# Joined edits to a three-block transformer kernel: two matmuls for three in the down projections, token-major groups in the last block, side jobs in half steps

## The chip, the cores and the metric

The kernel runs on one core of one Trainium2 chip. The metric is the device time of one execution in microseconds. The kernel before took 1733.04 us (median of 3 runs, 1731.53 to 1735.68).

## What is computed

Three transformer blocks follow each other on one sequence of 256 tokens (272 in the first block, with 16 meta tokens) of width 1024, in fp32. Cut to what matters:

```python
# first block: latent attention, then a gated linear recurrence
h = h + mla_mixer(rmsnorm(h, a_norm_g), ...)       # 8 heads, low-rank q and kv
r = sigmoid(uc @ w_rg + b_rg); i = sigmoid(uc @ w_ig + b_ig)
log_a = -8 * r * softplus(-lam); a = exp(log_a)
mult = sqrt(-expm1(2 * log_a))                     # 1 at the first token
b = mult * (i * uc)                                # then h_t = a_t * h_(t-1) + b_t
h = h + (scan(a, b) * silu(gate)) @ w_out
# second block, two layers: sparse attention, two convolution branches, a gated sum, an ffn
x = x + merged @ w_o
x = x + (silu(u_gate) * u_val) @ w_down            # 2816 wide
# third block
ret = silu(rg) * retention(rq, rk, rv)             # normalised per head of 256
mix = sigmoid(ga) * (ret @ w_ret_out) + sigmoid(gb) * (moba_attention(mq, mk, mv) @ w_moba_out)
x = x + mix @ w_o
x = x + (silu(h2 @ w_ffn_gate) * (h2 @ w_ffn_up)) @ w_ffn_down
```

## The kernel before

**Precision.** Weights and activations are fp32, and each is split into a high part of TensorE's fast type and a low rest. A product is then three matmuls (mm3): high by high, low weight by high activation, high weight by low activation. ScalarE (ACT) makes the high part of every piece of weight (whi, L175), VectorE (DVE) the rest (wlo, L181); in some stages a DMA issued by GpSimd (POOL) makes the rest instead.

**Units.** Weights come in units of 128x1024 elements (512 KB), in the order in which they are used. A dry run of the program records that order; in the second, a unit is loaded, and its split emitted, three units ahead of its use (AHEAD = 3).

**Two layouts of a product.** Feature-major (tile_fm): the weight's 128x128 piece is the stationary operand and 256 or 272 tokens move; one unit (8 pieces over k) makes one output tile of 128 features, in 24 matmuls of 256 columns. Token-major (tok_group, proj_tok): the activation's 128 tokens are stationary and 512 weight columns move; a unit holds two k, and makes 12 matmuls of 512 columns into two accumulators, one for each half of the tokens. Transposes on TensorE (to_fm, L858) bring a token-major result back.

**Side jobs.** Everything that is no large product (norms, heads of an attention, convolution taps) is a Python generator. `spawn` starts one with a rate; each unit of the main products calls `tick`, which advances every job by its rate in steps; `drain` runs a job to its end at once. `stagger` runs several heads at once, each some steps behind the other. An instruction's place on its engine's queue is then set by the scheduler of the tile framework; the queues run in order.

**The places that the change touches.** (1) `residual` runs an output projection over 8 tiles and adds it to x; called for the down projections of the two layers with kt = 22 k-pieces (w_dn), whose operands are fz, three pairs of tiles fh and fl. The third block's down projection (w_d3, L1543) is written out apart. (2) `mla`: heads are advanced at L655 to L670, then w_a_out starts with `lead`, the first k-pieces of four tiles, and `between` drains the heads. (3) `lru`, the recurrence: `block` makes the gates r and i by Sigmoid (L719), `gates` does Exp (L709) and Tanh (L711), a Sqrt over two tiles follows (L725), and `chain` multiplies on DVE (L740) and on POOL (L743) and scans (L747). (4) `third`: w_g3 makes the gate of the retention (8 tiles) and the two mixing gates (8 tiles each) feature-major, each scaled by the row rb of inverse norms; `retain` transposes its heads (L1466); `moba` makes the attention's heads from transposed probabilities (pt, ptb) and v (mo, L1418).

```python
    def tick(self, n=1.0):
        for job in list(self.jobs):
            job[2] += job[1] * n
            while job[2] >= 1.0 and job in self.jobs:
                job[2] -= 1.0
                self.step(job)
```

## Time and profile before

| | |
|---|---|
| median of 3 runs | 1733.04 us |
| profiled execution: its own time | 1733.38 us |
| its span (first to last instruction) | 1731.3 us |
| TensorE (PE) busy | 1709.9 us, 99% |
| DVE busy | 1365.5 us, 79% |
| ACT busy | 1068.0 us, 62% |
| POOL busy | 61.7 us, 4% |
| granted TensorE clock, mean | 0.999 |

Matmuls are pipelined: a row says 0.28 us for a matmul of 256 columns, but the next one starts 0.12 us later. What a matmul costs in a stream is the distance from its start to the next one's start, and that is read from a timeline or from a first and a last start with their count. "busy" can hide short gaps for the same reason; the waits are read from the view of waits and from the timeline.

### The profile page before, as it was taken

What the parts mean: (1) busy time and instruction counts of PE and PEld (TensorE: products, weight loads), DVE (VectorE), ACT (ScalarE), POOL (GpSimd) and SP (SyncE); (2) the same over time, 40 slices, a digit from 0 to 9 for tenths busy, and PEclk for the clock granted to TensorE, in tenths of its full rate; (3) what the DMA queues carried; (4) which work ended last, traced back from release to release, by engine and by line L of the source; (5) the groups of instructions that cost most, each with busy time, mean ns of one, the idle gap of its engine ahead of it and who ended that gap; (6) DMA issues with size and microseconds to landing.
All of it is one profiled execution on the core that took longest, in us unless ns stands there. A gap on an engine that the chain in (4) does not pass through costs nothing.

```text
span 1731.3 us, 31869 instructions
## 1 busy us (share of the span) xinstructions
PE 1709.9 (99%) x12215; PEld 1622.9 (94%) x12215; DVE 1365.5 (79%) x2943; ACT 1068.0 (62%) x1808; POOL 61.7 (4%) x92
## 2 busy tenths in 40 slices
PE   9999899999999999999999999999999999999999
PEld 8999899998888999999999888999998789999999
DVE  7769998998997998667998898898757677786553
ACT  5667775677656776546578557576545756455442
POOL 1000100000000000000000000000000000000000
PEclk9999999999999999999999999999999999999999
DMA  7425465776775555667686775656665436656563
GB/s 271 135 71 170 133 204 177 218 221 195 230 227 176 191 180 181 184 175 210 190 228 196 214 222 189 202 171 197 186 191 187 146 96 187 189 163 196 184 184 97
DMA packets 91545, 318.64 MB, mean 184 GB/s; under 512 B 10448, under 2 KB 11616, under 8 KB 91392
## 3 DMA queue, kind: packets, MB, share of 16 engines
q1 hardware_dynamic: 84384, 292.51, 53.1%
q0 software_dynamic: 7008, 24.09, 7.0%
q8 instruction: 96, 1.57, 0.4%
q14 instruction: 57, 0.47, 0.1%
HBM read 293.96 MB, written 1.05 MB: 170 GB/s over the span
## 4 chain that ended last, share of the span: by engine, by line
PE 92%; ACT 3%; DVE 2%; issue 1%; DMA 1%; SPq 0%; DVEq 0%; POOLq 0%; ACTq 0%
PE acc L205 22%; PE acc L207 22%; PE acc L206 21%; PE tok L207 7%; PE tok L205 7%; PE tok L206 7%; DVE wlo L181 1%; ACT whi L175 1%; PE lg L1115 1%; PE ix L1070 1%; PE po L1108 1%; DMA wlo<-raw 1%; ACT ca L1234 0%; DMA raw<-w_a_in 0%; PE pt L913 0%
## 5 line engine op out<-in xcount | busy, mean ns | idle before, releaser
L175 ACT ACTIVATE whi<-raw 128x1024 fp32r<-128x1024 f32 (+3 forms) x573 | 586.4, 1027 | 417.1 <-PE acc L207 170.3
L181 DVE TENSOR_TENSOR wlo<-raw,whi 128x1024 fp32r<-128x1024 f32 (+3 forms) x531 | 628.3, 1186 | 203.6 <-ACT whi L175 199.3
L205 PE MATMUL acc<-bh,whi 128*128 128x256 f32 x1600 | 459.1, 288 | 0.0
L206 PE MATMUL acc<-bh,wlo 128*128 128x256 f32 x1600 | 451.7, 283 | 0.0
L207 PE MATMUL acc<-bl,whi 128*128 128x256 f32 x1600 | 451.2, 283 | 0.0
L205 PEld LDWEIGHTS acc<-bh,whi 128*128 128x128 f32 x1600 | 306.8, 192 | 2.7 <-issue 1.4
L206 PEld LDWEIGHTS acc<-bh,wlo 128*128 128x128 f32 x1600 | 306.6, 192 | 2.2 <-issue 0.7
L207 PEld LDWEIGHTS acc<-bl,whi 128*128 128x128 f32 x1600 | 306.1, 192 | 0.2 <-DVE bl L158 0.2
L979 DVE SCALAR_TENSOR_TENSOR ca<-apad,vec,ca 128x226 f32<-128x226 f32 (+14 forms) x480 | 195.9, 460 | 0.3
L206 PE MATMUL acc<-ah,wlo 128*128 128x256 f32 (+1 forms) x528 | 151.5, 287 | 6.1 <-DVE wlo L181 6.1
L205 PE MATMUL acc<-ah,whi 128*128 128x256 f32 (+1 forms) x528 | 153.3, 290 | 1.5 <-ACT ah L161 1.1
L207 PE MATMUL acc<-al,whi 128*128 128x256 f32 (+1 forms) x528 | 151.5, 287 | 0.0
L205 PE MATMUL acc<-fh,whi 128*128 128x256 f32 x528 | 149.4, 283 | 0.0
L206 PE MATMUL acc<-fh,wlo 128*128 128x256 f32 x528 | 149.4, 283 | 0.0
L207 PE MATMUL acc<-fl,whi 128*128 128x256 f32 x528 | 149.4, 283 | 0.0
L206 PEld LDWEIGHTS acc<-ah,wlo 128*128 128x128 f32 x528 | 101.2, 192 | 7.1 <-DVE wlo L181 7.0
L205 PEld LDWEIGHTS acc<-ah,whi 128*128 128x128 f32 x528 | 101.2, 192 | 2.3 <-ACT ah L161 1.3
L205 PE MATMUL tok<-whi,ah 128*128 128x424 f32 (+1 forms) x272 | 102.7, 377 | 0.0
L205 PEld LDWEIGHTS acc<-fh,whi 128*128 128x128 f32 x528 | 101.4, 192 | 0.0
L206 PEld LDWEIGHTS acc<-fh,wlo 128*128 128x128 f32 x528 | 101.4, 192 | 0.0
L207 PEld LDWEIGHTS acc<-fl,whi 128*128 128x128 f32 x528 | 101.4, 192 | 0.0
L207 PEld LDWEIGHTS acc<-al,whi 128*128 128x128 f32 x528 | 101.1, 192 | 0.2 <-DVE al L162 0.2
(559 smaller groups left out, 3332.8 us busy)
## 6 DMA issues: line engine op xcount, KB each, us to landing
raw<-w_up SPq DMA_DIRECT2D x88, 512.0 KB, 3.9
raw<-w_g SPq DMA_DIRECT2D x72, 512.0 KB, 4.4
raw<-w_c SPq DMA_DIRECT2D x48, 512.0 KB, 4.5
raw<-w_f SPq DMA_DIRECT2D x44, 512.0 KB, 3.6
wlo<-raw POOLq DMA_DIRECT2D x36, 512.0 KB, 6.6
raw<-w_t SPq DMA_DIRECT2D x40, 424.0 KB, 3.2
raw<-w_a SPq DMA_DIRECT2D x32, 512.0 KB, 4.4
raw<-w_dn SPq DMA_DIRECT2D x32, 512.0 KB, 3.6
```

The source lines that it names most:

```text
L175: nc.scalar.activation(hi[:, c], raw[:, c], AF.Copy)
L181: nc.vector.tensor_sub(lo[:, c], raw[:, c], hi[:, c].bitcast(F32))
L205: mm(out, wh, xh, start=start, stop=False)
L206: mm(out, wl, xh, start=False, stop=False)
L207: mm(out, wh, xl, start=False, stop=stop)
L979: tap = dve.scalar_tensor_tensor(ca[:, i, d:], ga[:, i, :T - d], w(i, j), ca[:, i, d:], op0=ALU.mult, op1=ALU.add)
L1070: te.matmul(ps[:, n * 2 * nk:(n + 1) * 2 * nk].rearrange("p (h k) -> p h k", h=2), kiT[:, 2 + i, q], kiT[:, 6:8, :nk], start=True, stop=True)
L1108: te.matmul(po, tok[k][:, 584 + g * 128:584 + (g + 1) * 128], ptb[:, k * n:(k + 1) * n], start=k == 0, stop=k == j)
L1115: te.matmul(ps[:, i * nk:(i + 1) * nk], qT[:, h, q], kiT[:, g, :nk], start=True, stop=True)
```

## The change

Seven edits, made together:

1. The three down projections issue two matmuls for each k-piece where there were three: the high weight by high and low activation side by side (512 columns, into the two halves of a bank), and the low weight by the high activation (256 columns, into the first half). The two halves are then added by two DVE additions where there was one. The activation's parts are stored in pairs (class Pairs) for it.
2. In the third block, w_g3, w_mo and w_ro are token-major; the inverse norm is then a scale for each partition in the activation that empties the accumulator, and the row rb isn't made. The retention stays token-major (ry), is multiplied by its gate, and is transposed after that; the mixed sum is transposed too (mixture), before w_o3, which starts with `lead=(4, 4)`.
3. proj_tok and tok_group call `tick(0.5)` after each k instead of `tick()` after each two.
4. One `step(heads)` less ahead of w_a_out.
5. In `lru`, Sigmoid is written as a Tanh of half the argument, with the factors moved into scales and biases; the product of L743 moves from POOL to DVE.
6. The second sum of rows of the latent norm takes an accumulator of the products' pool instead of the pool of one tile.
7. In the third block, the first group of projections is emptied only after the norm's job is drained.

```diff
+    def wide_part(self, o, unit, xs, k0, k1, kt, base=0):
+        wh, wl = unit
+        mm = self.nc.tensor.matmul
+        for k in range(k0, k1):
+            x = xs(k)
+            c = slice((k - base) * 128, (k - base + 1) * 128)
+            mm(o, wh[:, c], x, start=k == 0, stop=k == kt - 1, skip_group_check=True)
+            mm(o[:, 0], wl[:, c], x[:, 0], start=False, stop=k == kt - 1, skip_group_check=True)
+        self.tick((k1 - k0) / 8)
...
-                r = yield from self.rows(r6[:, 3 * a:3 * a + 3], SEG1, "rb_l%d" % a)
+                r = yield from self.rows(r6[:, 3 * a:3 * a + 3], SEG1, "rb_l%d" % a,
+                                         self.acc("rlp") if a else None)
...
         self.step(heads)
-        self.step(heads)
         self.residual("w_a_out", 8, lambda k: (oh[:, k], ol[:, k]), h, T1, 0, ["b_norm_g"],
                       lead=(4, 5), between=lambda: self.drain(heads))
...
+            if wide:
+                o = next(first) if m < nl else self.wide_fm(name, m, kt, xw, n)
+                dve.tensor_add(src, o[:, 1], src)
+                o = o[:, 0]
...
-                dst, b = (rr, "b_b_rg") if c < 2 else (ii, "b_b_ig")
-                self.late(act.activation(dst[:, i], o, AF.Sigmoid, bias=self.v(b, i)))
+                dst, b = (rr, 0) if c < 2 else (ii, 8)
+                self.late(act.activation(dst[:, i], o, AF.Tanh, scale=0.5,
+                                         bias=self.hb[:, b + i:b + i + 1]))
...
-                dve.memset(rr[:, i, 0:1], 1.0)
-                pool.tensor_mul(ii[:, i], ii[:, i], rr[:, i])
+                dve.memset(rr[:, i, 0:1], 0.5)
+                dve.tensor_mul(ii[:, i], ii[:, i], rr[:, i])
...
                     self.mm3(a[j], xh[:, s], xl[:, s], wh[:, c], wl[:, c], k == 0, k == kt - 1)
-            self.tick()
+                self.tick(0.5)
...
-            pt = self.acc("rt")
-            for i in range(2):
-                for j in range(2):
-                    te.transpose(pt[:, i * 256 + j * 128:i * 256 + j * 128 + 128],
-                                 y[:, j * 256 + i * 128:j * 256 + i * 128 + 128], self.ident)
...
+        for g in range(2):
+            o = self.tok_group("w_g3", g, 8, xs)
+            for j in range(2):
+                act.activation(gr[:, j, g * 512:g * 512 + 512], o[j], AF.Copy,
+                               scale=self.rcol[:, j:j + 1])
...
+            for m in range(0, 8, 2):
+                c = slice(m * 128, m * 128 + 256)
+                dve.tensor_mul(ry[:, :, c], ry[:, :, c], gr[:, :, c])
                 yield
+                self.to_fm(ry, m, rT_h, rT_l)
+                yield
...
+        self.residual("w_o3", 8, lambda k: (mh[:, k], ml[:, k]), x, T, 0, ["norm2_w_3"],
+                      lead=(4, 4), between=lambda: self.drain(rjob))
...
-            o = self.tile_fm("w_d3", m, 22,
-                             lambda k: (fz[k // 8][0][:, k % 8], fz[k // 8][1][:, k % 8]), T)
-            dve.tensor_add(x[:, m], o, x[:, m])
+            o = self.wide_fm("w_d3", m, 22, lambda k: fz[k // 8](k % 8), T)
+            dve.tensor_add(x[:, m], o[:, 1], x[:, m])
+            dve.tensor_add(x[:, m], o[:, 0], x[:, m])
```

What this does to the order on the engines, at three places. The first is DVE in the recurrence, from the second product of L740 to the first weight rest behind it. Before (uc is the scan's result, gy the gate branch, ii and rr the gates):

```order
L740 SCALAR_TENSOR_TENSOR rr<-aa,rr 128x272 x2
L742 MEMSET rr 128x1
L747 SCALAR_TENSOR_TENSOR uc<-aa,ii 128x272
L742 MEMSET rr 128x1
L740 SCALAR_TENSOR_TENSOR rr<-aa,rr 128x272
L747 SCALAR_TENSOR_TENSOR uc<-aa,ii 128x272
L712 TENSOR_TENSOR ii<-ii,uc 128x272 x2
L742 MEMSET rr 128x1
L747 SCALAR_TENSOR_TENSOR uc<-aa,ii 128x272
L181 TENSOR_TENSOR wlo<-raw,whi 128x1024
```

And on the same engine at the same place of the changed kernel (L802 is the product of L740, L805 the one that was on POOL, L809 the scan, L197 the weight's rest):

```order
L802 SCALAR_TENSOR_TENSOR rr<-aa,rr 128x272
L833 TENSOR_TENSOR gy<-acc,nb_1934 128x256
L805 TENSOR_TENSOR ii<-ii,rr 128x272
L804 MEMSET rr 128x1
L802 SCALAR_TENSOR_TENSOR rr<-aa,rr 128x272
L805 TENSOR_TENSOR ii<-ii,rr 128x272
L772 SCALAR_TENSOR_TENSOR ii<-ii,uc 128x272 x2
L809 SCALAR_TENSOR_TENSOR uc<-aa,ii 128x272 x2
L197 TENSOR_TENSOR wlo<-raw,whi 128x1024
```

Two scans stand ahead of the weight's rest where there were three, and one product of L740 less; two products that POOL did stand there instead.

The second is TensorE near the end of the third block's attention, in the last group of projections (pt are transposes of probabilities, mo the product with v that needs their copy). Before:

```order
L205 MATMUL tok<-whi,ah 128x512
L206 MATMUL tok<-whi,al 128x512
L207 MATMUL tok<-wlo,ah 128x512
L913 MATMUL pt<-ident,p 128x128 x2
L1418 MATMUL mo<-ptb,rotmv 128x256
L913 MATMUL pt<-ident,p 128x128
```

In the changed kernel, from the same transposes on:

```order
L975 MATMUL pt<-ident,p 128x128 x2
L221 MATMUL tok<-whi,ah 128x512
L222 MATMUL tok<-whi,al 128x512
L223 MATMUL tok<-wlo,ah 128x512
L221 MATMUL tok<-whi,ah 128x512
L222 MATMUL tok<-whi,al 128x512
L223 MATMUL tok<-wlo,ah 128x512
L1488 MATMUL mo<-ptb,rotmv 128x256
```

Six matmuls of 512 columns stand between the transposes and the product where there were none; at the other pairs there are five to seven.

The third is TensorE at the start of w_a_out (acc<-oh is its product, pa and pb transposes of a head, po the head's product with v). Before:

```order
L590 MATMUL pa<-ident,p_1348 128x128
L598 MATMUL po<-pt_1459,qv 128x256
L599 MATMUL po<-pt,vt 128x256
L600 MATMUL po<-pt,vt 128x128
L586 MATMUL pb<-ident,p_1424 128x128
L588 MATMUL pa<-ident,p_1424 128x128
L205 MATMUL acc<-oh,whi 128x272
```

In the changed kernel:

```order
L641 MATMUL pa<-ident,p_1350 128x128
L221 MATMUL acc<-oh,whi 128x272
L222 MATMUL acc<-oh,wlo 128x272
L649 MATMUL po<-pt_1461,qv 128x256
L223 MATMUL acc<-ol,whi 128x272
```

The head's first product moved behind two matmuls of w_a_out; the second, third and the next head's transposes come twelve matmuls of it later.

## Rows read from the trace of the kernel before

**Rows 1.** The page's busy times: engine, us busy, share of the span, instructions.

```profile
PE 1709.9 (99%) x12215; PEld 1622.9 (94%) x12215; DVE 1365.5 (79%) x2943; ACT 1068.0 (62%) x1808; POOL 61.7 (4%) x92
```

**Rows 2.** The chain that ended last, share of the span by engine.

```profile
PE 92%; ACT 3%; DVE 2%; issue 1%; DMA 1%; SPq 0%; DVEq 0%; POOLq 0%; ACTq 0%
```

**Rows 3.** Waits of PE in the whole span: us in total, times, longest.

```profile
PE acc L206 <- DVE wlo L181: 6.9, 5, 3.1
PE mo L1418 <- ACT ptb L917: 3.0, 2, 1.6
PE acc L207 <- DVE yl L162: 1.3, 1, 1.3
...
PE po L598 <- DVE pt L594: 0.9, 1, 0.9
```

**Rows 4.** Instructions on fh from 1663.5 us on: durations, first and last start.

```profile
L205 PE MATMUL acc<-fh,whi x176: 283/283/283, 1664.1 to 1727.1; 128*128 128x256 f32 x176
```

**Rows 5.** Timeline of PE in w_ao of layer 1: start, us, instruction.

```profile
1007.66 0.39 PE L206 MATMUL tok<-whi,ol 128*128 128x512 f32 x1
...
1010.84 0.39 PE L205 MATMUL tok<-whi,oh 128*128 128x512 f32 x1
```

**Rows 6.** Timeline of PE from w_co to w_o of layer 0.

```profile
551.89 0.39 PE L207 MATMUL tok<-wlo,ch 128*128 128x512 f32 x1
552.12 0.28 PE L205 MATMUL acc<-mh,whi 128*128 128x256 f32 x1
552.23 0.28 PE L206 MATMUL acc<-mh,wlo 128*128 128x256 f32 x1
```

**Rows 7.** Timeline of PE around transposes in w_o of layer 0.

```profile
557.87 1.04 PE L858 MATMUL tr<-ident,mg 128*128 128x128 f32 x8
558.66 0.36 PE L205 MATMUL acc<-mh,whi 128*128 128x256 f32 x1
558.86 0.28 PE L206 MATMUL acc<-mh,wlo 128*128 128x256 f32 x1
```

**Rows 8.** Windows in the recurrence: us, then busy of PE, PEld, DVE, ACT, POOL; clock, DMA.

```profile
175.00:216.00 41.00, 33.96 (x260) 32.59 (x259) 37.25 (x71) 30.52 (x50) 7.84 (x8) 0.96 0.40 129
185.00:190.00 5.00, 4.82 (x28) 4.83 (x29) 3.86 (x9) 4.81 (x10) 0.00 (x0) 0.66 0.63 195
```

**Rows 9.** Timeline in the recurrence, DVE and POOL.

```profile
198.55 0.44 DVE L740 SCALAR_TENSOR_TENSOR rr<-aa,rr 128x272 f32<-128x272 f32 x1
...
198.79 0.83 POOL L743 TENSOR_TENSOR ii<-ii,rr 128x272 f32<-128x272 f32 x1 [14.75 <-ACT whi L175]
198.90 1.02 DVE L740 SCALAR_TENSOR_TENSOR rr<-aa,rr 128x272 f32<-128x272 f32 x1
...
202.34 1.77 DVE L181 TENSOR_TENSOR wlo<-raw,whi 128x1024 fp32r<-128x1024 f32 x1
...
204.38 1.21 DVE L181 TENSOR_TENSOR wlo<-raw,whi 128x1024 fp32r<-128x1024 f32 x1
```

**Rows 10.** Timeline at the recurrence's first wait, DVE and PE.

```profile
178.03 0.43 DVE L740 SCALAR_TENSOR_TENSOR rr<-aa,rr 128x272 f32<-128x272 f32 x1
...
182.78 0.71 DVE L747 TENSOR_TENSOR_SCAN uc<-aa,ii 128x272 f32<-128x272 f32 x1
...
183.41 1.71 DVE L181 TENSOR_TENSOR wlo<-raw,whi 128x1024 fp32r<-128x1024 f32 x1
...
185.18 0.38 PE L206 MATMUL acc<-ah,wlo 128*128 128x256 f32 x1 [1.88 <-DVE wlo L181]
```

**Rows 11.** A group of table loads of ACT, 155 to 215 us.

```profile
L719 ACT ACT_TABLE_LOAD x2 | 2.6, 1283 | 0.0
```

**Rows 12.** Timeline of PE in the third block's attention.

```profile
1376.71 0.38 PE L913 MATMUL pt<-ident,p 128*128 128x128 f32 x2
...
1378.88 0.70 PE L1418 MATMUL mo<-ptb,rotmv 128*128 128x256 f32 x2 [1.36 <-ACT ptb L917]
```

**Rows 13.** Timeline of the end: the last addition.

```profile
1727.66 0.42 DVE L1546 TENSOR_TENSOR x<-acc,x 128x256 f32<-128x256 f32 x1 [7.49 <-PE acc L207]
```

More of the change, by code (lines that the diff above doesn't have):

```diff
@@ L72, in __exit__, with __init__, __call__, parts @@
         return False
+class Pairs:
+    def __init__(self, prog, name, t):
+        self.a = [prog.big(name + "%d" % i, 8, t, F32R) for i in range(2)]
+    def __call__(self, k):
+        i = 2 * (k % 4)
+        return self.a[k // 4][:, i:i + 2]
+    def parts(self, k):
+        i = 2 * (k % 4)
+        return self.a[k // 4][:, i], self.a[k // 4][:, i + 1]
 class Prog:
@@ L224, in tile_fm, with wide_fm, wide_lead @@
         return o
+    def wide_part(self, o, unit, xs, k0, k1, kt, base=0):
[7 more added lines that the diff above has]
+        self.tick((k1 - k0) / 8)
+    def wide_fm(self, name, m, kt, xs, t):
+        o = self.acc()[:, :2 * t].rearrange("p (a t) -> p a t", a=2)
+        for k0 in range(0, kt, 8):
+            k1 = min(kt, k0 + 8)
+            self.wide_part(o, self.unit(name, m, k0 * 128, (k1 - k0) * 128), xs, k0, k1, kt, k0)
+        return o
+    def wide_lead(self, name, ms, xs, t, ks, between=None):
+        os = [(self.acc()[:, :2 * t].rearrange("p (a t) -> p a t", a=2),
+               self.unit(name, m, 0, 1024)) for m in ms]
+        for o, u in os:
+            self.wide_part(o, u, xs, 0, ks, 8)
+        if between:
+            between()
+        for o, u in os:
+            self.wide_part(o, u, xs, ks, 8, 8)
+            yield o
     def lead_fm(self, name, ms, xs, t, ks, between=None):
@@ L682, in residual @@
         nl = lead[0] if kt == 8 else 0
-        first = self.lead_fm(name, range(nl), xs, n, lead[1], between)
+        wide = isinstance(xs, list)
+        if wide:
+            xw = lambda k: xs[k // 8](k % 8)
+            first = self.wide_lead(name, range(nl), xw, n, lead[1], between)
+        else:
+            first = self.lead_fm(name, range(nl), xs, n, lead[1], between)
         for m in range(8):
-            o = next(first) if m < nl else self.tile_fm(name, m, kt, xs, n)
             src = x[:, m, t0:]
+            if wide:
+                o = next(first) if m < nl else self.wide_fm(name, m, kt, xw, n)
+                dve.tensor_add(src, o[:, 1], src)
+                o = o[:, 0]
+            else:
+                o = next(first) if m < nl else self.tile_fm(name, m, kt, xs, n)
             dve.tensor_add(src, o, src)
@@ L1333, in third, with group @@
         t1 = [self.big("t1_%d" % j, 1, 2048)[:, 0] for j in range(2)]
-        def group(g):
+        os = []
+        def group(g, wait=True):
             if g < 4:
@@ L1482, in norm @@
             self.norm_cols("n31")
-            yield
-            return (yield from self.rows(self.rcol, SEG2, "rb31"))
         job = self.spawn(norm(), 0.7)
-        group(0)
+        group(0, wait=False)
+        self.drain(job)
+        evict(0)
         group(1)
-        rb = self.drain(job)
         ajob = self.spawn(attention(), 1.2)
@@ L1514, in third @@
         mh, ml = self.big("mh", 8, T, F32R), self.big("ml", 8, T, F32R)
+        mixed = [0]
         for b, (wn, kt) in enumerate((("w_mo", 4), ("w_ro", 8))):
             ys = (lambda k: (rT_h[:, k], rT_l[:, k])) if b else (lambda k: (bT_h[:, k], bT_l[:, k]))
-            for m in range(8):
-                o = self.tile_fm("w_g3", 16 - 8 * b + m, 8, xs, T)
-                g = self.small("g3")[:, :T]
-                dve.tensor_mul(g, o, rb)
-                act.activation(g, g, AF.Sigmoid)
-                if b == 0 and m == 0:
+            for g in range(2):
+                c = slice(g * 512, g * 512 + 512)
+                o = self.tok_group("w_g3", 4 - 2 * b + g, 8, xs)
+                sgs = [self.half_k("sgt") for _ in range(2)]
+                for j in range(2):
+                    act.activation(sgs[j], o[j], AF.Sigmoid, scale=self.rcol[:, j:j + 1])
+                if b == 0 and g == 0:
@@ L1534, in third @@
-        fz = [(self.big("fh", 8, T, F32R), self.big("fl", 8, T, F32R)) for _ in range(3)]
+                if b == 1 and g == 0:
+                    self.drain(rjob)
+                    rjob = self.spawn(self.mixture(mg, mixed, mh, ml))
+                o = self.tok_group(wn, g, kt, ys)
+                for j in range(2):
+                    if b == 0:
+                        dve.tensor_mul(mg[:, j, c], o[j], sgs[j])
+                    else:
+                        dve.tensor_mul(sgs[j], o[j], sgs[j])
+                        dve.tensor_add(mg[:, j, c], mg[:, j, c], sgs[j])
@@ L1536, in finish @@
+                mixed[0] = b * (g + 1)
+        self.residual("w_o3", 8, lambda k: (mh[:, k], ml[:, k]), x, T, 0, ["norm2_w_3"],
+                      lead=(4, 4), between=lambda: self.drain(rjob))
+        fz = [Pairs(self, "f", T) for _ in range(3)]
         def finish(og, ou, i):
@@ L1686, in pack @@
                                     w[:, 1024:2048]], 1), 512)
[L1687 to L1689 removed]
+    d["w_g3"] = _tm(np.concatenate([w[:, 2048:3072], w[:, 4608:6656]], 1), 512)
+    d["w_ro"] = _tm(a["w_ret_out_3"][0], 512)
+    d["w_mo"] = _tm(a["w_moba_out_3"][0], 512)
     d["w_o3"] = _fm(a["w_o_3"][0])
```

74 lines of the change are left out of this document (30 added, 44 removed).

## The prediction

> **What bounds the kernel now.** I read the page's busy times and the chain first: PE is busy 99% of the span and is 92% of the chain, DVE is busy 79%, ACT 62% [rows 1, 2]. So the reader should see a kernel whose time is TensorE's stream of matmuls plus the gaps in that stream, and expect an edit to count only if it shortens the stream or closes a gap. The view of waits gives the gaps: 6.9 us for weight rests that DVE makes, 3.0 us for copied probabilities in the third block's attention, 1.3 us for the gated operand yl, 0.9 us in the first block's heads [rows 3]. Then I read what one matmul costs in the stream. In the last down projection 176 steps of three matmuls start between 1664.1 and 1727.1 us: 63.0 us over 175 steps is 0.360 us a step, 0.120 us for a matmul of 256 columns [rows 4]. In a token-major group 14 matmuls start between 1007.66 and 1010.84 us: 3.18 / 14 = 0.227 us for 512 columns [rows 5]. The 256 columns more cost 0.107 us, so about 13 ns of each matmul do not depend on its columns.
>
> **The down projections.** There are 528 k-pieces: 3 projections, 8 tiles, 22 pieces; rows 4 hold the last 176. A step was 0.360 us; with one matmul of 512 and one of 256 columns it is 0.227 + 0.120 = 0.347 us. 528 x 0.013 = 6.9 us less. This supposes that widths can alternate freely; where the trace has one change from 512 to 256, the wide one takes 0.23 us and the next 0.11 us [rows 6], so nothing is added there. The second addition in each tile is DVE work beside TensorE, which needs 22 x 0.347 = 7.6 us a tile, against 0.42 us for an addition [rows 13]; only the last tile's is on the path: +0.4 us.
>
> **Token-major in the third block.** w_g3 has 24 units, w_ro 8 and w_mo 8 half units: 36 units. One was 24 x 0.120 = 2.88 us and is 12 x 0.227 = 2.72 us. 36 x 0.156 = 5.6 us less. The mixed sum is now transposed, 16 transposes more; 8 of them take 0.79 us to the next matmul [rows 7], so +1.6 us. The gated heads keep their 16. The sum of rows for rb falls away, two small matmuls: I take 0.4 us, by four passes of a transpose's length.
>
> **Switches.** The first split matmul after a transpose takes 0.20 us where a stream has 0.12 [rows 7]. By the order of PE there are 14 more switches between split matmuls and others, so 7 more returns: 0.6 us at 0.08 each, 1.4 us at the whole 0.20. I take 1.0 us.
>
> TensorE's stream is then shorter by 6.9 + 5.6 - 1.6 + 0.4 - 1.0 = 10.3 us.
>
> One rule speaks against this. The Trainium skill, "TensorE: Matmul & The Clock Gate", section "Back-to-back issue gap", gives a lone matmul N / 2.4 + 2.5 ns at the full clock, a fixed part of 2.5 ns where the rows here leave 13 ns. By it the 528 matmuls saved in the down projections and the 432 in the third block would be worth an estimated 2.4 us in place of 12.5 us. The trace does not agree: by the page 256 columns would take 109 ns, and they take 120 ns.
>
> **The recurrence.** From 175 to 216 us PE is busy 33.96 of 41 us, DVE 37.25 [rows 8]. Three weight rests and the operand yl come late; the waits are most of the 6.9 us and all of the 1.3 us [rows 3]. After the first one the granted clock is 0.66 over 185 to 190 us [rows 8]: two thirds of that stretch at the lower level, 1.2 GHz, which costs 0.34 of 5 us, 1.7 us. What is late is DVE: beside a POOL product the same DVE product takes 1.02 us for 0.44 us, and a weight rest 1.77 us for 1.21 us [rows 9], about 0.55 us each; POOL makes eight products, so 8 x 0.55 = 4.4 us of DVE go when they move. They come back as eight DVE products at 0.35 us from start to start [rows 9]: 2.8 us. DVE is 1.6 us better off. ACT loads tables three times less (the order has 21 loads for 24), 3 x 1.28 = 3.8 us [rows 11], so the roots that DVE waits for come earlier.
>
> At the first wait the order tells more. The rest that PE needs starts 5.38 us after the second product of L740, at 183.41 us [rows 10]. Now that product, six other operations at 0.35 and two scans at 0.63 us (182.78 to 183.41) stand ahead, 3.7 us; so it starts 1.7 us earlier, and ends 0.5 us earlier again since no POOL product runs beside it. That covers the 1.88 us of PE's wait [rows 10], if ACT is in time. The later ones improve less, since DVE is nearly full: at the last operand three more small products stand ahead of yl. All gaps here, the waits and the slow clock, are at most 6.9 + 1.3 + 1.7 = 9.9 us; if DVE simply stays full, nothing of it goes. I take 3.5 us: 1.8 of the first wait, half of the slow clock, and 0.9 of the rest.
>
> **The third block's attention.** Two waits of the mo product cost 3.0 us [rows 3]. In one the transposes start at 1376.71 and the product at 1378.88 us [rows 12]: 2.17 us, in which ACT copies. Nothing of the main stream stood between. Now six matmuls do, 6 x 0.227 = 1.36 us, so of 1.36 us of wait nearly all is covered there. ACT is the engine that could take it back; I take 2.4 us, bounds 0 and 3.0.
>
> **The heads of the first block.** The product po waited 0.9 us [rows 3]. Now two matmuls stand ahead of it and twelve behind it, ahead of the parts that need later copies. I take 0.6 us, bounds 0 and 0.9.
>
> **Edits at nothing.** Half ticks in the two middle layers: none of PE's larger waits stands in their token-major groups [rows 3], and DVE is 21% idle over the span [rows 1]; without that cover a tap of the convolution placed ahead of a weight rest would cost its own length. The latent norm's second accumulator: it removes a wait for a buffer, worth less than what I can tell. Emptying the first group later: what is queued behind it on ACT is the split of units three ahead, 3 x 2.7 us of cover. Fewer and larger loads of w_mo: none of PE's larger waits is for a load [rows 3].
>
> **The sum.** -10.3 - 3.5 - 2.4 - 0.6 + 0.4 = -16.4 us. The profiled execution took 1733.4 us (span 1731.3 and 2.1 us around it), 0.3 us above the median: 1717.0 us.
>
> **The rivals.**
> *The waits stay.* DVE remains full in the recurrence and ACT in the attention, so that only the stream shortens: 1733.4 - 10.3 + 0.4 = 1723.5 us. For it: DVE is busy 37.25 of 41 us and gains only 1.6 us [rows 8, 9]. Against: the first wait is a matter of order, and the order is better.
> *All the waits go.* The recurrence gives 9.9 us, the attention 3.0, the heads 0.9: 1733.4 - 10.3 - 13.8 + 0.4 = 1709.7 us. For it: both full engines get relief. Against: DVE's share.
> *The fixed part isn't paid by the matmul.* The 13 ns could belong to something that the merged matmul pays as well, such as reading its operand; then a wide step stays at 0.360 us and a group gains nothing: 1717.0 + 12.5 = 1729.5 us. Against: 0.227 us for 512 columns is not twice 0.120 us [rows 4, 5]. The page's rule lies close to this case.
> *Alternating widths cost (slower).* No row shows a stream in which 512 and 256 columns take turns on one bank. If each change of width cost what the return from transposes costs, 0.08 us [rows 7], 2 x 528 changes would cost 84 us: 1717.0 + 84 = 1801 us. It decides from 16.4 / 1056 = 16 ns a change on. Against: one change at no cost [rows 6].
> *The merge does nothing.* If the three matmuls were bound by the weight's stream and not by TensorE, fewer of them would change nothing; PE's 99% and the short list of waits leave little room for it.
>
> **How the numbers follow.** The forecast case 0.60, with its own range 1713 to 1721 us. The waits stay 0.18, all go 0.11, fixed part not saved 0.05, alternating widths 0.03, no effect 0.03. A change is told from none by about 0.2%, 3.5 us. Faster: the first four cases, 0.94. Same: 0.03. Slower: 0.03. The range takes in the second and third case, 1709 to 1725 us, and leaves out 0.11.
>
> **What would show it.** Down projections: 0.347 us a k-piece, 61.0 us for the last 8 tiles where there were 63. Third block: 128x512 rows at 0.227 us for w_g3, w_mo and w_ro, 32 more transposes of tr less 16 of rt. Recurrence: L740's product at 0.44 us throughout, four table loads, no stretch at a clock under 0.9, waits on weight rests in the whole span of 4 to 5 us in place of 6.9. Attention: no wait of mo over 0.5 us. It would be wrong if the wide step took 0.36 us or more, or if a new wait stood in the third block's mixing, where DVE now sums 512 columns at a time and w_o3 waits for the transposes.

## The result and the profile after

The changed kernel took 1721.01 us (median of 4 runs, 1720.09 to 1722.51), the kernel before 1733.52 us beside it (4 runs, 1731.53 to 1735.68): a ratio of 0.9931, 95% interval 0.9919 to 0.9943. So the change is faster by 12.5 us, 3.9 us less than the 16.4 us that the sum gave: inside the stated range, 1709 to 1725 us, and at the upper end of the forecast case's own, 1713 to 1721 us. The profiled execution spans 1719.0 us, 12.3 us less than the one before, so the two profiles tell the same story as the runs. Of all the runs below one, of the kernel with two steps of the heads, took 2065.87 us where its others took 1721 to 1725, and is left out as slow.

The page of the changed kernel, busy times and then the shares of the chain, which answer to [rows 1, 2]:

```profile
PE 1704.5 (99%) x11267; PEld 1574.2 (92%) x11267; DVE 1360.6 (79%) x2922; ACT 1065.0 (62%) x1784; POOL 54.5 (3%) x84
...
PE 90%; ACT 4%; DVE 3%; DMA 1%; issue 1%; SPq 0%; POOLq 0%; ACTq 0%; DVEq 0%
```

TensorE still bounds the kernel, with 948 matmuls fewer; a per cent or two of the chain went from it to ACT and DVE.

To see where the time went I took the starts of the same matmuls in both traces (the first product on a new operand of the main stream, or the first of a norm's sum) and wrote down how much less time the changed kernel took between them:

| stretch | forecast, us | changed kernel |
|---|---|---|
| start to the norm ahead of the recurrence (heads, latent norm) | -0.6 | -0.8 |
| that norm to the norm behind the recurrence | -3.5 | -4.6 |
| layers 0 and 1 outside the down projections | 0 | +1.7 |
| three down projections | -6.9 | -3.5 |
| third block from its first projection to its last norm | -5.8 | -5.3 |
| last addition | +0.4 | +0.4 |

The third block's forecast is -5.6 + 1.6 - 0.4 + 1.0 - 2.4. Before rounding the rows add up to the 12.3 us of the span. Two of them missed: the down projections gave half, and layer 0 took back 1.7 us where nothing was expected. The recurrence gave 1.1 us more than expected in this execution.

TensorE's waits over the whole span, as in [rows 3]:

```profile
PE acc L223 <- DVE yl L178: 2.5, 1, 2.5
PE acc L221 <- ACT ah L177: 1.2, 1, 1.2
...
PE acc L221 <- ACT oh L177: 0.8, 1, 0.8
PE tok L223 <- DMA wlo<-raw: 0.8, 2, 0.5
PE acc L222 <- DVE wlo L197: 0.7, 2, 0.5
PE mups L1271 <- DVE lnst L1049: 0.5, 1, 0.5
...
PE mo L1488 <- ACT ptb L979: 0.2, 1, 0.2
```

The waits that the forecast closed are nearly closed: weight rests of DVE fell from 6.9 to 0.7 us in the products by feature, mo from 3.0 to 0.2, and po isn't in the list. The operand yl grew from 1.3 to 2.5 us, the wait for rests that a DMA makes from 0.2 to 0.8 us, and one for oh of 0.8 us is new.

The down projection of layer 0 in the changed kernel, instructions on f and then some in order of time (start, us, instruction):

```profile
L250 PE MATMUL acc<-f,whi x176: 395/398/403, 700.8 to 762.6; 128*128 128x512 f32 x176
L251 PE MATMUL acc<-f,wlo x176: 277/281/284, 701.0 to 762.8; 128*128 128x256 f32 x176
```

```profile
704.17 0.28 PE L251 MATMUL acc<-f,wlo 128*128 128x256 f32 x1
704.28 0.40 PE L250 MATMUL acc<-f,whi 128*128 128x512 f32 x1
704.52 0.28 PE L251 MATMUL acc<-f,wlo 128*128 128x256 f32 x1
704.64 0.40 PE L250 MATMUL acc<-f,whi 128*128 128x512 f32 x1
704.88 0.28 PE L251 MATMUL acc<-f,wlo 128*128 128x256 f32 x1
```

From 704.17 to 704.88 us are two k-pieces: 0.355 us each. Over the 176 pieces, from the first wide start to the first product of the next stage, it is 62.19 us, 0.3534 us a piece: a wide matmul is followed after 0.236 us and a narrow one after 0.117 us on the mean. Forecast were 0.227 and 0.120. No wait stands between them, so the 0.006 us is a price of the stream itself.

The recurrence, in windows of the stretch of [rows 8] (us; busy of PE, PEld, DVE, ACT, POOL; clock, DMA):

```profile
175.00:190.00 15.00, 15.00 (x128) 15.00 (x127) 14.96 (x35) 14.95 (x28) 0.00 (x0) 1.00 0.44 127
190.00:200.00 10.00, 9.94 (x83) 9.53 (x81) 9.98 (x22) 9.96 (x15) 0.00 (x0) 1.00 0.52 164
200.00:204.00 4.00, 1.04 (x3) 0.44 (x3) 4.00 (x11) 1.50 (x3) 0.00 (x0) 1.00 0.94 322
204.00:208.00 4.00, 3.98 (x20) 3.98 (x21) 4.00 (x12) 1.09 (x3) 0.00 (x0) 0.57 0.10 41
208.00:212.00 4.00, 4.00 (x36) 4.00 (x35) 3.40 (x6) 0.75 (x2) 0.00 (x0) 1.00 0.49 128
```

Up to 200 us TensorE now has almost no gap. DVE is full up to 208 us, and what it is late with stands at the end: TensorE has 1.04 us of work from 200 to 204 us, and after that pause the granted clock is 0.57, most of 204 to 208 us at the lower level, 1.2 GHz.

### The profile page after: what moved, and what is told of

Same layout as the page of the kernel before. It is cut to its first block, busy times and chain, and to the rows that moved or that the text cites. A ratio compares the mean times of both kernels' runs of the same rounds, so it can differ in the third digit from the quotient of the medians.

```text
span 1719.0 us, 29881 instructions
## 1 busy us (share of the span) xinstructions
PE 1704.5 (99%) x11267; PEld 1574.2 (92%) x11267; DVE 1360.6 (79%) x2922; ACT 1065.0 (62%) x1784; POOL 54.5 (3%) x84
## 4 chain that ended last, share of the span: by engine, by line
PE 90%; ACT 4%; DVE 3%; DMA 1%; issue 1%; SPq 0%; POOLq 0%; ACTq 0%; DVEq 0%
PE acc L221 16%; PE acc L223 16%; PE acc L222 16%; PE tok L223 9%; PE tok L221 9%; PE tok L222 9%; PE acc L250 7%; PE acc L251 4%; DVE wlo L197 1%; ACT whi L191 1%; PE lg L1177 1%; PE ix L1132 1%; PE po L1170 1%; DMA wlo<-raw 1%; ACT ca L1296 0%
## 5 line engine op out<-in xcount | busy, mean ns | idle before, releaser
L197 DVE TENSOR_TENSOR wlo<-raw,whi 128x1024 fp32r<-128x1024 f32 (+3 forms) x527 | 626.7, 1192 | 207.5 <-ACT whi L191 202.2
L250 PE MATMUL acc<-f,whi 128*128 128x512 f32 x528 | 186.7, 399 | 0.0
L251 PE MATMUL acc<-f,wlo 128*128 128x256 f32 x528 | 148.3, 281 | 0.0
L221 PE MATMUL tok<-whi,ah 128*128 128x512 f32 (+1 forms) x368 | 142.4, 387 | 0.0
L223 PE MATMUL tok<-wlo,ah 128*128 128x512 f32 (+1 forms) x368 | 138.3, 376 | 0.0
L222 PE MATMUL tok<-whi,al 128*128 128x512 f32 (+1 forms) x368 | 138.0, 375 | 0.0
L250 PEld LDWEIGHTS acc<-f,whi 128*128 128x128 f32 x528 | 99.2, 188 | 24.7
L251 PEld LDWEIGHTS acc<-f,wlo 128*128 128x128 f32 x528 | 99.7, 189 | 0.0
L221 PE MATMUL acc<-ah,whi 128*128 128x272 f32 (+1 forms) x336 | 98.1, 292 | 1.2 <-ACT ah L177 1.2
L222 PE MATMUL acc<-ah,wlo 128*128 128x272 f32 (+1 forms) x336 | 97.1, 289 | 0.3 <-DVE wlo L197 0.2
L223 PE MATMUL acc<-al,whi 128*128 128x272 f32 (+1 forms) x336 | 96.9, 288 | 0.0
```

The source lines that it names most:

```text
L197: nc.vector.tensor_sub(lo[:, c], raw[:, c], hi[:, c].bitcast(F32))
L221: mm(out, wh, xh, start=start, stop=False)
L222: mm(out, wl, xh, start=False, stop=False)
L223: mm(out, wh, xl, start=False, stop=stop)
L250: mm(o, wh[:, c], x, start=k == 0, stop=k == kt - 1, skip_group_check=True)
L251: mm(o[:, 0], wl[:, c], x[:, 0], start=False, stop=k == kt - 1, skip_group_check=True)
```

## The experiments

The ratios are to runs of the kernel before on the same chip (medians 1732.2 to 1733.4 us). "c" is the first product on the convolution's output, "z" that on the attention's output of a middle layer; from z to c lie w_so, its gates, w_ao and the side work of the convolution. The landing of a DMA is the time from its issue until its data have arrived.

### Widths in blocks

```diff
-            mm(o[:, 0], wl[:, c], x[:, 0], start=False, stop=k == kt - 1, skip_group_check=True)
+        for k in range(k0, k1):
+            c = slice((k - base) * 128, (k - base + 1) * 128)
+            mm(o[:, 0], wl[:, c], xs(k)[:, 0], start=False, stop=k == kt - 1,
+               skip_group_check=True)
```

> The changed kernel, with the eight wide products of a unit first and its eight narrow ones behind them, so that the width changes twice in a unit and not sixteen times. In the changed kernel a down projection takes 62.19 us, 0.3534 us a k-piece, where I had 0.347; the wide start is followed after 0.236 us, the narrow one after 0.117 us. Theory 'changing width costs': wide 0.227 to 0.230 and narrow 0.120, 0.347 to 0.350 us a piece, 61.1 to 61.6 us a projection, 1.8 to 3.4 us less in all: 1717.6 to 1719.2 us. Rival 'this wide product costs 0.236 us wherever it stands' (its operand of two rows, or its output): 0.236 + 0.120 = 0.356 us, 62.6 us a projection, 1722 us.

Measured: 1718.58 us (1717.72 to 1723.76), ratio 0.9924 [0.9912, 0.9937]. A projection takes 61.49 us, 0.70 us less, in all three of them. The same view as above, of this kernel:

```profile
L250 PE MATMUL acc<-f,whi x176: 389/393/398, 700.2 to 760.7; 128*128 128x512 f32 x176
L253 PE MATMUL acc<-f,wlo x176: 277/283/283, 702.0 to 761.6; 128*128 128x256 f32 x176
```

So the width's changes cost, and the rival falls. The starts show how: in each of the 72 blocks, to within 2 ns, the intervals from the first wide matmul on are 233, 236, 228, 233, 231, 227, 227 and 227 ns, and from the first narrow one 113, 119 and then 120 ns. The price sits behind a change from 256 to 512 columns, 26 to 28 ns over five matmuls, and the change back returns 8 ns. The trace of the kernel before had it, at the start of the third block, where the last down projection ends:

```profile
1301.11 0.28 PE L207 MATMUL acc<-fl,whi 128*128 128x256 f32 x1
1301.23 0.40 PE L205 MATMUL tok<-whi,ah 128*128 128x512 f32 x1
1301.47 0.40 PE L206 MATMUL tok<-whi,al 128*128 128x512 f32 x1
1301.70 0.39 PE L207 MATMUL tok<-wlo,ah 128*128 128x512 f32 x1
1301.93 0.40 PE L205 MATMUL tok<-whi,ah 128*128 128x512 f32 x1
1302.16 0.39 PE L206 MATMUL tok<-whi,al 128*128 128x512 f32 x1
1302.39 0.39 PE L207 MATMUL tok<-wlo,ah 128*128 128x512 f32 x1
```

From 1301.23 to 1302.39 us five matmuls take 1.16 us where the settled cadence gives 5 x 0.227 = 1.135.

### Fewer changes of width

This kernel also uses half ticks in the third block alone, as a run below does.

```diff
-        for k in range(k0, k1):
...
+        for w in ((0, 1), (1, 0))[k0 // 8 % 2]:
+            for k in range(k0, k1):
+                c = slice((k - base) * 128, (k - base + 1) * 128)
+                if w == 0:
+                    mm(o, wh[:, c], xs(k), start=k == 0, stop=k == kt - 1, skip_group_check=True)
+                else:
+                    mm(o[:, 0], wl[:, c], xs(k)[:, 0], start=False, stop=k == kt - 1,
+                       skip_group_check=True)
```

> As the run before last of the wide products (blocks by unit, half ticks in the third block alone), with the order of the second unit of a tile turned round: wide, narrow, narrow, wide, wide, narrow. In the block order the intervals behind a change from 256 to 512 columns are 233, 236, 228, 233 and 231 ns, then 227; behind a change from 512 to 256 they are 113 and 119 ns, then 120. So a pair of changes costs 26 to 28 ns and gives 8 back. Theory 'each pair of changes costs about 20 ns': three pairs a tile become two, 8 x 0.020 = 0.16 us less a projection, 61.33 us in place of 61.49, 0.5 us in all: 1716.6 us. Rival 'the pattern goes by the place in the unit and not by the change': 61.49 us stays.

Measured: 61.33 us for each of the three projections, as the theory had it to the digit. The median is 1719.10 us (1717.71 to 1720.09), ratio 0.9921 [0.9907, 0.9934], not the 1716.6 expected: in its profile layer 0 takes 1.6 us more than in the kernel it is compared with, a loss that the next point follows.

### Ticks by halves and by wholes

In both token-major helpers, for the changed kernel with whole ticks (and with the signs turned for the kernel before with half ticks):

```diff
-                self.tick(0.5)
+            self.tick()
```

> The changed kernel, with the side jobs advanced by whole units again in both token-major helpers. The changed kernel loses 1.75 us between 478 and 525 us in w_so and its gates of layer 0, where rests made by a DMA of POOL's queue land 8.1 to 10.2 us after their issue; layer 1 loses nothing at the same place. Theory 'the half ticks put the side work so that the DMA's transfer or its issue comes late': no wait for a DMA's rest there, 1.75 us back; and in the third block's attention the product mo waits about 1.4 to 2.4 us again, so about the same time in all, 1721 to 1722 us. Rival 'the kernel comes there 5.5 us earlier, and the transfers meet others': the 1.75 us stay, 1722 to 1723 us. Rival 'landing times differ from run to run': either.

> The kernel before, with only the half ticks. Theory 'half ticks cost in layer 0': 1 to 2 us lost between w_ao and w_co of layer 0, with waits for rests made by a DMA, none in layer 1, and the waits of mo in the third block's attention (3.0 us) fall to under 1 us, since products of the main stream now stand between its transposes and mo: 1731 to 1733 us. Rival 'earlier arrival': nothing lost in layer 0, 1731 us. Rival 'the attention's gain comes from the token-major blocks around it and not from the half ticks': mo still waits 2 to 3 us.

The third block first. The wait of mo in the changed kernel with whole ticks, and in the kernel before with half ticks:

```profile
PE mo L1488 <- ACT ptb L979: 3.0, 2, 1.6
```

```profile
PE mo L1418 <- ACT ptb L917: 0.2, 1, 0.2
```

The half ticks alone close that wait. Put into the kernel before they shorten the span by 2.1 us, 2.0 of it between the third block's first projection and the end of its attention, and the time is 1729.97 us (1729.21 to 1732.0), ratio 0.9985 [0.9977, 0.9994]. Taken from the changed kernel they cost 1.7 us there: 1723.17 us (1720.7 to 1725.16), ratio 0.9943 [0.9929, 0.9956]. The rival, that the token-major blocks did it, falls.

In layer 0, from z to c, the changed kernel takes 116.07 us and the kernel before 114.32. With whole ticks it is 114.55 us, and with the half ticks in the kernel before 114.08: neither alone makes the loss. The next two runs carry this on.

```diff
-                self.tick(0.5)
+                if self.fine:
+                    self.tick(0.5)
+            if not self.fine:
+                self.tick()
...
+        self.fine = True
```

> The changed kernel, with the wide products of a unit ahead of its narrow ones, and half ticks in the third block alone. The block order gave 0.70 us a projection, 2.1 us. Theory 'half ticks cost in layer 0 and help in the third block': 114.0 to 114.5 us between the two marks of layer 0 in place of 115.55 us, and mo waits 0.2 us: 1.0 to 1.5 us less than with the block order alone, 1717.3 us. Rival 'landing of the DMA's rests differs from run to run': 114.0 to 116.1 us, and 1718.6 us.

Measured: 1717.07 us (1716.22 to 1720.61), ratio 0.9911 [0.9898, 0.9924], with 114.01 and 114.03 us from z to c in the two layers: the shortest time of all. That fits the theory of the half ticks, but the kernel of the turned order has the same ticks, and its layer 0 takes 115.65 us. So I ran the changed kernel once more:

> The changed kernel once more, unchanged, for what differs from run to run. In its trace the rests made by DMA in w_so and the gates of layer 0 land 9.6 and 10.2 us after their issue, and the stretch takes 116.07 us; in a kernel where they land within 8.7 us it takes 114.0 us, and in one with the same half ticks within 8.6 us 114.1 us. Theory 'the landing differs from run to run, and the half ticks only leave less room': another time than 116.07 us, between 114.1 and 116.1, with landing times that go with it. Rival 'the order fixes it': 115.9 to 116.2 us again. Time 1721 us, within 1.

Measured: 1722.65 us (1720.45 to 1724.08), ratio 0.9939 [0.9927, 0.9952]. The same kernel's two medians, 1721.01 and 1722.65 us, are 1.6 us apart, so a smaller difference between two medians here says little. Layer 0 takes 114.59 us this time, and layer 1, which had lost nothing, 116.79 us. So the loss isn't fixed by the order of instructions. It goes with the landing of the rests made by DMA. The rows of that DMA's issue line give their count and their time to landing; the changed kernel, layer 0:

```profile
L195 POOL DMA_DIRECT2D wlo<-raw x5: 869/869/869, 444.7 to 488.2; - x5
...
DMA to landing us min/median/max: 5.0/8.1/10.2
```

the same kernel once more, layer 1:

```profile
L195 POOL DMA_DIRECT2D wlo<-raw x4: 872/872/874, 989.3 to 1023.1; - x4
...
DMA to landing us min/median/max: 8.5/9.5/9.7
```

and the one that lost nothing, layer 0:

```profile
L196 POOL DMA_DIRECT2D wlo<-raw x5: 872/872/872, 445.5 to 489.0; - x5
...
DMA to landing us min/median/max: 4.5/7.6/7.8
```

In the two layers 0 they are issued at the same moments after z; in layer 1 the first of them is, and the others come 0.8 to 1.4 us later, behind its late landing. With units split three ahead, in no layer whose longest landing is 9.3 us or less is more than 0.3 us lost against 114.03; with 9.6 and 10.2 us for the last two it is 2.0 us, with 9.8 and 10.6 us (turned order) 1.6 us. Of the 2.0 us the view of waits gives 0.8 to these rests; by the starts of the products the units that wait for them lose 1.4 us, since the matmuls behind a wait start late as well, and 0.6 us is lost at the norm's sum that comes behind them (the row lnst above).

It is not a matter of POOL's queue alone: the load of w_g issued 0.2 us behind the last of these rests lands after 10.6 us in the changed kernel and after 5.1 us in the one that lost nothing, and the three loads ahead of it were issued 0.3 to 1.2 us before that rest in the first and 2.4 to 3.3 us before it in the second. That fits transfers that slow each other when they come close together, and a late landing that pushes the next loads later; no run varied it.

What starts it stays open: four profiles of the kernel before and its variants have no stretch over 114.32 us, eight of nine of the changed kernel and its variants have one over 114.5, with whole ticks as with half. That may be more than chance, but no single part of the change explains it.

### More lead for the rests

```diff
-    AHEAD = 3
+    AHEAD = 4
```

> The kernel with block order and half ticks in the third block alone (1717.07 us), with weight units split four ahead of the one in use in place of three; a unit of the token-major stages takes 24 x 0.227 = 5.4 us. Over ten profiles of the changed kernel and its variants, the stretch from z to c of layers 0 and 1 takes 114.0 to 116.8 us and goes with the landing of the rests made by DMA: within 9 us of their issue nothing is lost, at 9.6 to 10.6 us 0.6 to 2.7 us. Theory 'the loss is that lateness alone': with 5.4 us more lead 114.0 to 114.3 us in both layers and no wait of TensorE for such a rest, whatever the landing; over several executions some 0.5 to 1.5 us less than before in this stretch. Against it in the sum: the rests that DVE makes stand one unit earlier in its queue, and in the recurrence, where DVE is busy 14.98 of 15 us, the operand yl can come 1 to 2 us later. Time 1716 to 1719 us. Rival 'the split waits for the buffer of the unit in use': no earlier issue, the waits stay, 1717 us or more.

Measured: 1724.44 us (1723.9 to 1725.79), ratio 0.9957 [0.9943, 0.9970]: 7 us slower than with three. In layer 0:

```profile
L196 POOL DMA_DIRECT2D wlo<-raw x5: 869/869/869, 449.4 to 492.9; - x5
...
DMA to landing us min/median/max: 4.6/5.9/6.2
```

and the waits of TensorE over the span:

```profile
PE tr L1125 <- DVE tok L952: 2.2, 2, 1.3
PE tok L222 <- ACT ch L174: 1.4, 2, 0.7
...
PE tok L223 <- DVE cl L175: 1.0, 2, 0.5
```

The waits for the DMA are gone, but not by more lead. These are the first products on z in layer 0 of the kernel with three ahead and of this one:

```profile
409.61 0.47 PE L222 MATMUL tok<-whi,zh 128*128 128x512 f32 x1
413.50 0.47 PE L222 MATMUL tok<-whi,zh 128*128 128x512 f32 x1
```

So the five rests are issued from 35.9 to 79.4 us after z in both kernels, and their units are used at the same moments too: no earlier issue, as the rival said. Each kind of weight tile has five buffers (bufs=5 in the kernel), and with three ahead the split already waits until TensorE is done with the unit five before. ACT at the last of these rests in that kernel:

```profile
486.70 1.06 ACT L192 ACTIVATE whi<-raw 128x1024 fp32r<-128x1024 f32 x1 [1.66 <-PE tok L223]
```

What is gone is the late landing: 6.2 us at most in this layer and 6.7 in layer 1. The weight loads do come earlier; none is issued within 3 us behind the last rest, where with three ahead one follows after 0.2 us. That may be the reason; it is not shown. (The 5.4 us in the expectation is two units; one is 12 x 0.227 = 2.7 us.) Against that stand new waits on ACT and DVE, 115.2 us from z to c in both layers, and 92.39 us in the recurrence in place of 89.56. So whether more lead would cure the lateness is not answered: this edit gave none, and cost 7 us.

### The recurrence

The kernel before with the hunks of `lru` and of its constants alone, and the changed kernel without them; then each half of the edit by itself:

> The kernel before, with only the recurrence's edit (Tanh in place of Sigmoid, no memory of table loads between, the product on DVE). From the traces the recurrence gained 4.5 us between the gates and the next norm. Theory 'all of it is this edit': 4.5 us by the next stage, 1729 us; rival 'the heads' order gave a part, since it moves what stands ahead of the first wait': 2 to 3.5 us, 1730 to 1731.5 us. In layer 0 'earlier arrival meets other transfers' expects a loss of 1 to 2 us between w_ao and w_co; 'half ticks' and 'run to run' expect none or either.

> The changed kernel, with the recurrence as it was before (Sigmoid, products on POOL). The recurrence's edit alone gave 3.6 us when it was put into the kernel before, and the changed kernel gained 4.5 us there. Theory 'the edit is worth 3.6 to 4.5 us wherever it stands': the stretch from the gates to the next norm is 3.6 to 4.5 us longer. Layer 0 loses 1.2 to 1.75 us between w_ao and w_co only where half ticks and the earlier arrival came together (the changed kernel and its block order, 116.07 and 115.55 us between two marks, against 114.03 to 114.55 us for the four others). Theory 'both are needed': 114.0 to 114.5 us here, so 1723 to 1724 us; rival 'half ticks with the other parts of the change are enough': 115.5 us or more, 1725 us.

```diff
-                dve.tensor_mul(ii[:, i], ii[:, i], rr[:, i])
+                pool.tensor_mul(ii[:, i], ii[:, i], rr[:, i])
```

> The changed kernel, with the product of the recurrence back on POOL and Tanh kept. Theory 'DVE's slowing beside POOL is what the waits were made of': the slow products of 1.02 us and rests of 1.77 us are back and with them the first wait for a weight rest of 1.9 us and more: 3 to 4 us lost of the 4.5, 1724 to 1725 us. Rival 'the three table loads made the roots late, and the gain is ACT's': at most 1 us lost, 1721 to 1722 us. Half of it each: 1723 us.

The kernel before, with the opposite edit:

```diff
-                pool.tensor_mul(ii[:, i], ii[:, i], rr[:, i])
+                dve.tensor_mul(ii[:, i], ii[:, i], rr[:, i])
```

> The kernel before, with the products of the recurrence on DVE in place of POOL and nothing else (Sigmoid stays, and with it the loads of tables). With Tanh and the products on POOL the changed kernel lost nothing in the recurrence: 89.2 us from the norm ahead of it to the norm behind it, against 88.8 to 90.0 us with the products on DVE, and 92.7 to 93.5 us with Sigmoid. Theory 'the three table loads are the whole gain': 92.7 to 93.8 us here, so 1732.5 to 1733.5 us. Rival 'DVE's slowing beside POOL is worth something where the roots are late': 90 to 92 us, 1730 to 1732 us.

From the norm ahead to the norm behind, with the tables' loads from 150 to 216 us:

| kernel | product | gate | loads | stretch, us | run, us |
|---|---|---|---|---|---|
| before | POOL | Sigmoid | 7 | 93.43 | 1733.5 |
| before, half ticks | POOL | Sigmoid | 7 | 93.49 | 1729.97 |
| changed, old recurrence | POOL | Sigmoid | 7 | 92.68 | 1724.28 |
| before, product moved | DVE | Sigmoid | 7 | 89.94 | 1729.56 |
| changed, product on POOL | POOL | Tanh | 4 | 89.18 | 1720.47 |
| before, new recurrence | DVE | Tanh | 4 | 89.94 | 1729.05 |
| changed; once more | DVE | Tanh | 4 | 88.80; 89.88 | 1721.01; 1722.65 |

Either half of the edit gives as much as both, 3.5 to 4 us (the move alone in the kernel before, Tanh alone in the changed one; the other two pairings were not run). The ratios of the four kernels, in the order of their expectations, are 0.9976 [0.9967, 0.9986], 0.9951 [0.9939, 0.9963], 0.9927 [0.9915, 0.9939] and 0.9982 [0.9973, 0.9991]. Both of my theories for the last two runs fall: with Tanh the return to POOL cost nothing, and without Tanh the move to DVE gave 3.5 us although the seven loads stayed. Layer 0 takes 114.03 us with the new recurrence in the kernel before, so arriving earlier alone loses nothing there; the changed kernel with the old one takes 115.09 us, between what the two theories of that run gave.

Windows of two kernels show what the gain stops at. The kernel before with the product on DVE:

```profile
175.00:185.00 10.00, 10.00 (x83) 9.78 (x82) 9.21 (x23) 9.93 (x18) 0.00 (x0) 1.00 0.31 79
...
205.00:230.00 25.00, 24.23 (x187) 24.23 (x188) 22.40 (x51) 15.01 (x31) 0.00 (x0) 0.93 0.40 125
```

The changed kernel with the product on POOL:

```profile
175.00:185.00 10.00, 9.76 (x81) 9.55 (x80) 9.64 (x23) 9.53 (x18) 3.00 (x4) 1.00 0.25 79
...
190.00:205.00 15.00, 11.59 (x90) 10.69 (x89) 14.66 (x29) 12.39 (x18) 3.29 (x4) 1.00 0.57 179
205.00:230.00 25.00, 24.22 (x194) 23.96 (x193) 23.33 (x49) 16.75 (x35) 0.25 (x1) 1.00 0.44 137
```

In both the first wait is gone: TensorE is busy 10.00 and 9.76 us from 175 to 185 us, where the kernel before has 8.30. Behind it DVE is full, and TensorE waits for it in one form or another: with the product on POOL 3.0 us for rests and 1.4 us for yl, in six pieces of at most 2.0 us, and the granted clock stays at 1.00; with both halves of the edit 0.5 and 2.5 us, and then 4 us at a clock of 0.57. So part of what both halves save in waits goes back to the slower clock; how much is not separated, since a slower TensorE also waits less for yl.

The length of a wait does not tell whether the clock falls behind it. The longest wait of the kernel before, and the window behind it:

```profile
204.17 0.39 PE L206 MATMUL acc<-ah,wlo 128*128 128x256 f32 x1 [3.05 <-DVE wlo L181]
204.00:208.00 4.00, 3.68 (x29) 3.48 (x29) 4.00 (x7) 0.45 (x2) 0.00 (x0) 1.00 0.61 186
```

The changed kernel with the old recurrence, at the same place:

```profile
201.20 0.58 PE L222 MATMUL acc<-ah,wlo 128*128 128x256 f32 x1 [3.05 <-DVE wlo L197]
201.00:205.00 4.00, 3.80 (x18) 3.80 (x18) 4.00 (x7) 0.71 (x2) 0.00 (x0) 0.50 0.64 164
```

The clock stays at 1.00 in the one and is 0.50 in the other. At the first wait it is the other way round: 0.66 behind 1.88 us in the kernel before, 1.00 behind 1.86 us here.

The stretch itself varies from 88.80 to 89.98 us over eight profiles with the same two edits. The longer ones have more of the lower clock behind the same wait of 2.5 us for yl. The changed kernel once more shows 0.50 from 204 to 208 us, and 0.77 in the 4 us behind it, which ran at 1.00 in the first profile:

```profile
204.00:208.00 4.00, 4.00 (x19) 4.00 (x20) 4.00 (x12) 1.09 (x3) 0.00 (x0) 0.50 0.12 49
208.00:212.00 4.00, 4.00 (x28) 4.00 (x28) 3.35 (x6) 0.75 (x2) 0.00 (x0) 0.77 0.52 143
```

### The heads

```diff
         self.step(heads)
+        self.step(heads)
         self.residual("w_a_out", 8, lambda k: (oh[:, k], ol[:, k]), h, T1, 0, ["b_norm_g"],
```

> The changed kernel, with the second step of the heads ahead of w_a_out again. Between the last products of the heads and the second half of the gates the changed kernel gained 0.8 us. Theory 'the order of po and of the first two products of w_a_out did it': the wait of po is back (0.9 us), the wait for oh (0.8 us) falls away or shrinks, 0.5 to 0.9 us lost there, which is within what the medians can tell: 1721 to 1722 us. Rival 'the step only moves the wait': under 0.2 us.

Measured: five runs of 1720.93 to 1725.12 us, ratio 0.9944 [0.9931, 0.9957]. The wait is back, and the one for oh is not in its list:

```profile
PE po L649 <- DVE pt L645: 0.9, 1, 0.9
```

From the first product on the latents to the norm ahead of the recurrence it takes 98.30 us, against 97.58 and 97.59 us in the two profiles of the changed kernel and 98.54 in the kernel before. So the step is worth 0.7 us by the traces, too little for these medians to confirm.

## Why the prediction was right, and where its sum was off

**TensorE's stream bounds the kernel.** Right: each shortening of the stream (1.17 us a projection, 0.70 us more by blocks, 0.16 us more by turning them) moved everything behind it by its own length.

**Down projections, -6.9 us.** Measured -3.5 us: the step that failed is "this supposes that widths can alternate freely ... so nothing is added there". I took the price from one change from 512 to 256 columns [rows 6], the direction that gives 8 ns back, and didn't read the one change the other way that the same trace has, at 1301.23 us. That direction costs 26 to 28 ns spread over five matmuls, and in a stream that alternates the net is 0.0064 us a k-piece: 528 x 0.0064 = 3.4 us, most of the 3.9 us by which the sum was off. The slower rival had the right mechanism at a twenty-fifth of its price: 3.2 ns a change where it took 80 and decided from 16.

**The fixed part.** The 13 ns is paid by each matmul, as the sum had it: with four changes of width a tile in place of 44, 176 pieces take 61.33 us where the three matmuls took 63.36: 2.0 us less, so the rival on the fixed part is out. By the rule for a lone matmul in the Trainium skill, "TensorE: Matmul & The Clock Gate", section "Back-to-back issue gap", it would be an estimated 176 x 2.5 ns = 0.4 us. The trace does not agree: it is the 2.0 us.

**Token-major in the third block, with the transposes and switches, -3.4 us.** Right. With whole ticks, where the attention gives nothing, the stretch is 3.6 us shorter.

**The third block's attention, -2.4 us.** Right in mechanism: 2.0 us alone and 1.7 us in the changed kernel, by the half ticks and not by the groups around them.

**The recurrence, -3.5 us.** Measured -4.6 us in the first profile and -3.5 us in the second, so the size held. The working was half right: the first wait goes, DVE stays full and yl comes later. But its parts came out otherwise: from 150 to 233 us the waits for rests fell from 5.7 to 0.5 us, where most of the later ones were to stay, yl took back 1.2 us, and the slow clock, which was to halve, came at another place. What the runs put in place of "DVE is 1.6 us better off" and the earlier roots is that either gave as much as both. Two signs were wrong: that no stretch would show a clock under 0.9, and that 4 to 5 us of waits for weight rests would be left (0.7 of the 6.9 us are).

**The heads, -0.6 us.** Measured -0.7. The latent norm's accumulator, costed at nothing, may be the remaining 0.2 us of that stretch (98.54 to 98.30); it was not tried alone, nor was the later emptying of the first group.

**Edits at nothing.** Half ticks in the two middle layers: the row of the table says +1.7 us, but the runs put it down to late landings that come and go, with whole ticks as with half, though in these profiles only in kernels with the change. That no larger wait stood there in [rows 3] was true; that rests made by DMA had little room left was not looked at.

**The total.** That it came within 4 us of the sum owes something to this execution: the 1.7 us of late landings and the 1.1 us more from the recurrence differ from one execution to the next, and here they partly cancel.

## What to carry to other kernels

Price a stream in which shapes take turns from both directions of a change, and over several instructions behind it, not from one neighbour. Two edits that relieve the same full engine need not add up: run each alone before adding them. A wait that shows in one profile and in the next moves to another layer is not fixed by the program: profile the unchanged kernel twice before explaining it. And after an edit that is to give more lead, read the moments of issue before judging it by the time.

## What the runs showed that was not expected

A change of the moving width acts on matmuls well behind it: 233, 236, 228, 233 and 231 ns and only then 227 ns, the same in 72 blocks of three projections, and 233, 236, 228, 233 and 231 ns once more at the one such place of the kernel before. It isn't bound to a change of width alone: where the stream of 512 columns starts again behind two products of the attention, at 1367.90 us of the kernel before, the intervals are 425, 233, 236, 224, 231, 236, 228, 233 and 231 ns, and then 226 and 227. Blocks of eight by width cost no room and gave 2.1 us in the trace, turning every second unit round another 0.5 us, and the kernel with the lowest median (blocks, half ticks in the third block) took 1717.07 us. And a wait of TensorE can cost more than its length, but not reliably: behind 3.05 us the clock stayed at 1.00 in one kernel and was 0.50 in another, and behind the same wait of 2.5 us it was 0.57 over the next 4 us in one execution, and 0.50 and then 0.77 over 8 us in the next.
